# A hand-ordered recurrent scan: the list of pieces rewritten, eight state updates summed on TensorE, zero fills moved to GpSimd

## The chip, the core and the metric

The kernel runs on one core of one Trainium2 chip. The metric is device time in microseconds (us) of one execution. The kernel before took 2023.44 us (median of 3 runs, 2020.06 to 2025.55).

## The reference, cut to what matters

One layer of a diffusion block over 512 latent tokens and 256 context tokens, width 1024. A token mixer runs first (a bidirectional delta-rule scan beside a spatial-gating branch, then gates and an output projection), and an expert-choice mixture of 16 SwiGLU experts after it. The part that is touched is the scan:

```
def step(S, inp):
    r_t, k_t, v_t, d_t, kk_t, a_t = inp
    s_kk = einsum('bhvk,bhk->bhv', S, kk_t)
    S_new = S * d_t - s_kk[..., None] * (kk_t * a_t) + v_t[..., None] * k_t
    y = einsum('bhvk,bhk->bhv', S if reverse else S_new, r_t)
```

It runs forward and backward, 16 heads of 64, first over the context from a zero state, then over the latents from the context's final state.

## The kernel before, in words

The scan is done in chunks of 64 tokens: 4 context steps (0 to 3) and 8 latent steps (4 to 11), each in both directions (d = 0, 1). A step with its direction is written `5.1`. What happens in one step is cut into pieces, each a short function. The order in which all pieces are issued is a string, `PLAN` with its tail `PLAN_END`, read from left to right. The letters:

- `l` (`prep_load`, line 652): loads of the chunk's operands, tiles `al` and `xx`, for both directions; 6 DMAs. In `al` each head pair has a half that must be zero; ScalarE writes it (line 659).
- `S`, `U`, `R` (lines 822 to 840): loads of v into the next state tile `sv` and into `uv`, and of the queries `ro`; 4 DMAs each.
- `a` (`prep`, line 672): 8 products on TensorE; ScalarE copies one part to `ap`, VectorE masks the other part into `al`. `o` stores `ap` to DRAM (4 DMAs).
- `v` (`wave`, line 714) begins a wave, which inverts the triangular blocks of two steps at once: it loads `Dt` from DRAM (the two `o` must have landed) and starts 31 rank-one steps, two VectorE instructions each (`rank1`, lines 710 and 712). `p n` (`pump`) issues n of them, and nothing where no wave is open. `F` issues what is left, and `D` stores the result (a VectorE copy at line 731, 2 DMAs). `i` (`wave_in`) loads it for one step (6 DMAs).
- `V`, `X` (`level`, `level2`): the off-diagonal blocks of the inverse. `K` transposes the keys into `bk`.
- `z`, `y`, `s`: the recurrence. `z` multiplies by the old state (ScalarE copies to `zn`), `y` by the inverse (ScalarE copies to `uv`), `s` gives the next state: TensorE's product is added to `sv` by VectorE (line 882) and scaled by `gC` (line 883), for two halves, so four VectorE instructions.
- `q`, `w`: the chunk's own scores and the outputs, in latent steps only. `h` are parts of the readout that follows.

SP, TensorE and ScalarE work in written order throughout, and within `PLAN` VectorE and GpSimd do as well. All loads are issued by SP's one queue, so a DMA that waits holds back those written behind it. Large tiles share 32 slots (`NBIG`, tag "big"), and a load waits until its slot is free. In the stage ahead of the scan, `HOOK` puts the first five loads, the first two waves and, at its end, `prep_load` 5 between projections. Behind the scan come the branch projections, the router, and then the experts, whose weights (`we`) are streamed from HBM.

A latent pair of steps in the old order reads as follows (step 6 and the start of step 7):

```
y5.0 y5.1 D3 i6 i7 s5.0 a8.0 a8.1 s5.1 o8 w5 l9 U6 V6 K6 X6 S7 z6.1 q6.0 q6.1 z6.0 a9.0 a9.1 o9 v4
R7 y6.0 y6.1 s6.0 s6.1 p8 w6 p4 U7 V7 K7 X7 p4 S8 z7.0 z7.1 p4 q7.0 q7.1 p8 l10 F4 R8 y7.0 y7.1 D4
```

Of the kernel before, what the change touches and what calls it, by code (L numbers as in the profile page):

```python
# [7 lines left out]
F32 = mybir.dt.float32  # L8
F32R = mybir.dt.float32r
I32 = mybir.dt.int32  # L10
AF = mybir.ActivationFunctionType
OP = mybir.AluOpType
# [5 lines left out]
KT = 8  # L18
# [3 lines left out]
C = 64  # L22
# [21 lines left out]
def block_kernel(es: ExitStack, tc, x, ctx, cT, ada_w, ada_b, pc, rows, w_ch, w_vs, w2, a2, g2, sgu_w,  # L44
                 wba, wbb, w_out, rw, e1, e3, e2, out):
    nc = tc.nc
    V, S, G, PE, SY = nc.vector, nc.scalar, nc.gpsimd, nc.tensor, nc.sync

    cp = es.enter_context(tc.tile_pool(name="const", bufs=1))
# [10 lines left out]
    def nm(p):  # L60
        cnt[0] += 1
        return f"{p}{cnt[0]}"

    def T(shape, name="t", dt=F32):
        return big.tile(shape, dt, name=nm(name), tag="big", bufs=NBIG)

    def K(shape, name="t", dt=F32):
        return keep.tile(shape, dt, name=nm(name), tag="keep", bufs=NKEEP)

    def P(name="p"):  # L70
        return pp.tile([128, 512], F32, name=nm(name), tag="ps")

    def mm(o, l, r, start=True, stop=True):
        PE.matmul(o, l, r, start=start, stop=stop, skip_group_check=True)  # L74
# [18 lines left out]
    ident = cp.tile([128, 128], F32, name="ident")  # L93
# [28 lines left out]
    zcol = zcol2[:, 0:1]  # L122
    gC = cp.tile([128, 2, NC, KT], F32, name="gC")

    def rstd(v, n, eps, scale=1.0):
        a = sm.tile([128, n], F32, name=nm("rv"), tag=f"rv{n}")
        y = sm.tile([128, n], F32, name=nm("ry"), tag=f"ry{n}")
        t = sm.tile([128, n], F32, name=nm("rt"), tag=f"rt{n}")
        V.tensor_scalar(a, v, scale, eps, op0=OP.mult, op1=OP.add)  # L129
        V.tensor_scalar(t.bitcast(I32), a.bitcast(I32), 1, None, op0=OP.logical_shift_right)  # L130
        V.tensor_scalar(y.bitcast(I32), t.bitcast(I32), -1, 0x5f3759df, op0=OP.mult, op1=OP.add)
        V.tensor_scalar(a, a, -0.5, None, op0=OP.mult)
        for _ in range(3):
            if n == 1:
                V.scalar_tensor_tensor(t, y, y, a, op0=OP.mult, op1=OP.mult)
            else:
                V.tensor_mul(t, y, y)
                V.tensor_mul(t, t, a)
            V.scalar_tensor_tensor(y, t, 1.5, y, op0=OP.add, op1=OP.mult)
        return y  # L140
# [129 lines left out]
    for d in range(2):  # L270
        for lst, src, nme in ((w2p, w2, "w2p"), (a2p, a2, "a2p")):
            t = T([128, D], nme)
# [34 lines left out]
    for k in range(KT):  # L307
# [5 lines left out]
        for (dst, i0, n, j) in ((hl(k), 2, 4, 0), (hc(k), 0, 2, 1)):  # L313
# [4 lines left out]
            t = T([128, TL], "hf")  # L318
# [314 lines left out]
    def cidx(si, d):  # L633
        lat, s = steps[si]
        n = NCL if lat else NCX
        return lat, (n - 1 - s if d else s)

    def uidx(si, d):
        lat, c = cidx(si, d)
        c += NCX if lat else 0  # L640
        return NC - 1 - c if d else c
# [4 lines left out]
    tmpi = cp.tile([128, 256], F32, name="tmpi")  # L646
    AL, XX, AP_, TP, X1, BK, RO, UV, SV = {}, {}, {}, {}, {}, {}, {}, {}, {}

    def halves(e):
        return (slice(0, 64), slice(64, 128)) if e == 0 else (slice(64, 128), slice(0, 64))  # L650

    def prep_load(si):
        for d in range(2):
            u = uidx(si, d)
            al = T([128, 2, KT, C], "al")
            xx = T([128, KT, 2, C], "xx")
            for e in range(2):
                own, oth = halves(e)
                S.activation(al[oth, e], zcol[oth, :, None].to_broadcast([64, KT, C]), AF.Copy)
                SY.dma_start(al[own, e], Ad_[d, :, own, u, :].rearrange("c p n -> p c n"))  # L660
            SY.dma_start(xx.rearrange("p c s n -> p c (s n)"),
                         Xd_[d, :, :, u].rearrange("c p s n -> p c (s n)"))
            AL[si, d], XX[si, d] = al, xx
# [8 lines left out]
    def prep(si, d):  # L672
        al, xx = AL[si, d], XX[si, d]
        if d == 0:
            AP_[si] = T([128, 2, KT, C], "ap")
        ap = AP_[si][:, d]
        for b in range(2):
            p = P("sc").rearrange("p (c e n) -> p c e n", c=4, e=2)
            for q in range(4):
                ct = 4 * b + q  # L680
                mm(p[:, q], xx[:, ct].rearrange("p s n -> p (s n)"), al[:, :, ct, :])
            cc = slice(4 * b, 4 * b + 4)
            for e in range(2):
                own, oth = halves(e)
                S.activation(ap[own, cc, :], p[own, :, e, :], AF.Copy)
            for e in range(2):
                own, oth = halves(e)
                V.tensor_tensor(al[oth, e, cc, :], p[oth, :, e, :],
                                mS[oth, None, :].to_broadcast([64, 4, C]), OP.mult)
# [162 lines left out]
    yt = [None] * 4  # L852
    QS = {}
# [19 lines left out]
    def state(si, d):  # L873
        bk, sv, uv, svn = BK.pop((si, d)), SV[si, d], UV[si, d], SV[si + 1, d]
        u = uidx(si, d)
        sp = P("sp").rearrange("p (c n) -> p c n", c=KT)
        for ct in range(KT):
            for e in range(2):
                mm(sp[halves(e)[0], ct], bk[:, ct, e, :], uv[:, e, ct, :])
        for e in range(2):  # L880
            own, _ = halves(e)
            V.tensor_tensor(svn[own, e], sp[own], sv[own, e], OP.add)
            V.tensor_tensor(svn[own, e], svn[own, e], gC[own, d, u, :, None].to_broadcast([64, KT, C]), OP.mult)

    def query(si, d):
        xx, ro = XX.pop((si, d)), RO[si, d]
# [10 lines left out]
    def why(si):  # L897
        got = []
        for d in range(2):
            lat, c = cidx(si, d)  # L900
            tt = c // 2
            if yt[tt] is None:
                yt[tt] = K([128, D], "y")
            got.append((RO.pop((si, d)), QS.pop((si, d)), SV.pop((si, d)), UV.pop((si, d)), yt[tt],
                        slice((c % 2) * 64, (c % 2) * 64 + 64), (c < NCL // 2) == (d == 0)))
        for b in range(2):
            ps = [P("yp") for _ in range(2)]
            for q in range(4):
                ct = 4 * b + q
                for e in range(2):  # L910
                    cs = slice(q * 128 + e * 64, q * 128 + e * 64 + 64)
                    for p, (ro, qs, sv, uv, _, hs, _) in zip(ps, got):
                        mm(p[hs, cs], ro[:, e, ct, :], sv[:, e, ct, :], start=True, stop=False)
                    for p, (ro, qs, sv, uv, _, hs, _) in zip(ps, got):
                        mm(p[hs, cs], qs[:, e, ct, :], uv[:, e, ct, :], start=False, stop=True)
            for p, (ro, qs, sv, uv, y, hs, first) in zip(ps, got):
                dst = y[hs, b * 512:b * 512 + 512]
                if first:
                    S.activation(dst, p[hs], AF.Copy)
                else:  # L920
                    V.tensor_tensor(dst, dst, p[hs], OP.add)
# [56 lines left out]
    def finish(_):  # L978
# [7 lines left out]
        ('s', 1): ((prep_load, 2), (pump, 4),),  # L986
        ('b', 0): ((prep_load, 3), (pump, 4),),
        ('a', 1): ((prep_load, 4), (finish, 0),),
        ('end', 0): ((prep_load, 5), (statics, 0),),
        ('u', 5): ((pump, 4),),  # L990
        ('u', 6): ((pump, 4),),
        ('u', 7): ((pump, 4),),
# [65 lines left out]
    for d in range(2):  # L1058
# [1 line left out]
            V.memset(SV[0, d][halves(e)[0], e], 0.0)  # L1060

    PLAN = (
# [9 lines left out]
    ).split()  # L1072
    PLAN_END = (
        "S11 z10.0 z10.1 q10.0 q10.1 h10.0 R11 y10.0 y10.1 s10.0 s10.1 p8 h10.1 w10 h10.2 p4 U11 V11 K11 X11 "
        "p4 z11.0 z11.1 p4 q11.0 q11.1 p8 h11.0 y11.0 y11.1 h11.1 w11 h11.2 "
    ).split()

    def finish_wave(w):
        while gens and waves and gens[0][0] == waves[0][0]:
            pump(1)  # L1080
# [478 lines left out]
    e, hidT = NE - 1, hidTs.pop(NE - 1)  # L1559
# [20 lines left out]
    with tc.manual_schedule():  # L1580
# [9 lines left out]
        r = rstd(mv[:, :, 1], 4, LN_EPS)  # L1590
# [70 lines left out]
```

## Time and profile before

| what | value |
|---|---|
| median of 3 runs | 2023.44 us (2020.06 to 2025.55) |
| the profiled execution, its own time | 2026.06 us |
| its span, first to last instruction | 2024.3 us |
| mean granted TensorE clock | 0.955 of full speed |
| TensorE busy | 1768.7 us (87%), 13216 matmuls |
| VectorE busy | 937.7 us (46%) |
| ScalarE busy | 619.8 us (31%) |
| GpSimd busy | 234.6 us (12%) |
| scan, from the first transposed keys to the last output | 582.0 to 910.8 us |

The span is one execution on the hardware profiler's clock. Busy times of different engines overlap, so they don't sum to the span. In rows of the profile, PE is TensorE, DVE VectorE, ACT ScalarE, POOL GpSimd and SP SyncE, whose queue (SPq) issues the DMAs; "x4" counts instructions, and what stands behind "<-" ended the engine's idle time.

### The profile page before, as it was taken

The numbers are of one execution on the slowest core, as the hardware profiler recorded it, in microseconds if no ns is written. First come the engines' busy times: TensorE is split into PE (matmuls) and PEld (weight loads), VectorE is DVE, ScalarE is ACT, GpSimd is POOL, SyncE is SP. The second block draws the span as 40 slices with busy tenths as digits, with TensorE's granted clock in tenths as the row PEclk, the third lists the DMA queues.
The fourth block names the chain that finished last, engine by engine and source line by source line (L and its number), as shares of the span: only waits on it lengthen the run. The fifth ranks groups of instructions, "written<-read, shape, count | busy, mean of one in ns | idle before, by whom it ended". The sixth has DMA issues, their size and how long they took to land.

```text
span 2024.3 us, 32347 instructions
## 1 busy us (share of the span) xinstructions
PE 1768.7 (87%) x13216; PEld 1134.4 (56%) x13216; DVE 937.7 (46%) x1695; ACT 619.8 (31%) x1057; POOL 234.6 (12%) x158
## 2 busy tenths in 40 slices
PE   5989999899988767687978999999998899999895
PEld 3877778778777767686964443434343243434334
DVE  6788885787836667887782111010201101020115
ACT  2777665443246645352331110100111010011101
POOL 4422224000100000044530000000000000000000
PEclk9999999899999888898978999999999999999998
DMA  9355567477785655484458999999999999999995
GB/s 324 115 172 172 177 189 240 145 229 229 247 234 130 143 135 135 109 235 159 142 232 353 426 427 427 426 427 427 427 427 427 426 427 426 427 427 427 427 424 209
DMA packets 364011, 592.41 MB, mean 293 GB/s; under 512 B 220372, under 2 KB 282068, under 8 KB 315736
## 3 DMA queue, kind: packets, MB, share of 16 engines
q1 hardware_dynamic: 363864, 590.35, 79.0%
q8 instruction: 104, 1.70, 0.3%
q14 instruction: 43, 0.35, 0.1%
HBM read 541.78 MB, written 47.71 MB: 291 GB/s over the span
## 4 chain that ended last, share of the span: by engine, by line
DMA 38%; PE 10%; DVE 4%; issue 0%; ACT 0%; DVEq 0%; SPq 0%
DMA we<-in_e 38%; PE hh L74 4%; PE yx L74 1%; PE co L74 1%; PE ye L74 1%; PE xe L74 1%; PE ba L74 1%; PE lg L74 1%; PE hT L1505 0%; DVE x L1245 0%; DVE wk L1423 0%; DVE m L1422 0%; DVE x L1253 0%; DVE x L1254 0%; DVE mt L1187 0%
## 5 line engine op out<-in xcount | busy, mean ns | idle before, releaser
L74 PE MATMUL hh<-we,xe 128*64 128x512 f32 x2048 | 461.4, 595 | 23.6 <-DMA we<-in_e 23.4
L74 PEld LDWEIGHTS hh<-we,xe 128*64 128x64 f32 x2048 | 149.0, 137 | 322.8 <-issue 261.9
L74 PE MATMUL ye<-we,hidT 128*64 128x512 f32 (+1 forms) x1216 | 253.6, 533 | 37.3 <-DMA we<-in_e 36.9
L1495 DVE TENSOR_TENSOR hd<-hd,hh 64x512 f32<-64x512 f32 x64 | 44.1, 690 | 516.6 <-ACT hd L1494 515.6
L74 PE MATMUL zl<-hL,H 128*128 128x512 f32 x816 | 261.1, 401 | 1.1 <-DVE hf L319 1.1
L74 PEld LDWEIGHTS ye<-we,hidT 128*64 128x64 f32 x1216 | 82.4, 136 | 199.7 <-DMA we<-in_e 106.3
L1494 ACT ACTIVATE hd<-hh 64x512 f32<-64x512 f32 x64 | 37.8, 591 | 490.7 <-PE hh L74 490.7
L74 PEld LDWEIGHTS zl<-hL,H 128*128 128x128 f32 x816 | 155.4, 193 | 30.0 <-issue 2.8
L74 PE MATMUL zl<-hL,L 128*128 128x512 f32 x408 | 163.0, 399 | 9.7 <-DVE L L160 9.7
L160 POOL TENSOR_TENSOR L<-w,H 128x1024 fp32r<-128x1024 f32 x54 | 138.2, 2566 | 208.9 <-ACT H L159 155.2
L159 ACT ACTIVATE H<-w 128x1024 fp32r<-128x1024 f32 x91 | 94.8, 1052 | 83.6 <-PE zl L74 25.1
L1588 POOL TENSOR_TENSOR x<-x,row 128x1024 f32<-128x1024 f32 x2 | 4.6, 2340 | 941.1 <-DVE rv L129 941.1
L1513 ACT ACTIVATE ye<-ye 64x512 f32<-64x512 f32 (+1 forms) x34 | 18.8, 554 | 271.6 <-PE ye L74 271.2
L1514 DVE SCALAR_TENSOR_TENSOR ye<-ye,gate,srow 64x512 f32<-64x512 f32 (+1 forms) x38 | 23.8, 663 | 148.4 <-ACT ye L1513 148.1
L74 PEld LDWEIGHTS zl<-hL,L 128*128 128x128 f32 x408 | 78.6, 193 | 21.8 <-DVE L L160 10.8
L710 DVE TENSOR_TENSOR tmpi<-Dt,Xt 128x31 f32<-128x31 f32 (+15 forms) x186 | 63.6, 342 | 19.7 <-DMA Dt<-Asd 14.1
L712 DVE TENSOR_TENSOR Xt<-Xt,tmpi 128x31 f32<-128x31 f32 (+15 forms) x186 | 63.8, 343 | 6.5
L74 PEld LDWEIGHTS xe<-oh,h 128*128 128x128 f32 x512 | 59.6, 196 | 8.9 <-issue 8.9
L74 PE MATMUL co<-ye,ohT 128*128 128x512 f32 (+1 forms) x144 | 64.4, 604 | 0.0
L74 PE MATMUL sc<-al,xx 128*128 128x128 f32 x384 | 49.6, 289 | 16.3 <-DMA xx<-Xkd 7.9
L74 PE MATMUL xe<-oh,h 128*128 128x128 f32 x512 | 61.8, 282 | 0.7 <-DVE oh L1446 0.7
L160 DVE TENSOR_TENSOR L<-w,H 128x1024 fp32r<-128x1024 f32 x37 | 46.7, 1263 | 31.1 <-ACT H L159 23.8
(322 smaller groups left out, 2914.5 us busy)
## 6 DMA issues: line engine op xcount, KB each, us to landing
we<-in_e SPq DMA_DIRECT2D x376, 1024.0 KB, 19.6
w<-in_w_ch SPq DMA_DIRECT2D x51, 512.0 KB, 4.9
w<-in_ada_w SPq DMA_DIRECT2D x32, 512.0 KB, 5.2
xx<-Xkd SPq DMA_DIRECT2D x28, 512.0 KB, 5.5
adaw<-in_ada_w SPq DMA_DIRECT2D x16, 512.0 KB, 10.3
we<-in_e SPq DMA_DIRECT2D x32, 256.0 KB, 5.5
Xkd<-g SPq DMA_DIRECT2D x32, 192.0 KB, 2.7
Ald<-al SPq DMA_DIRECT2D x16, 384.0 KB, 2.3
```

The lines of the kernel that those rows point to most:

```text
L74: PE.matmul(o, l, r, start=start, stop=stop, skip_group_check=True)
L159: S.activation(h, t, AF.Copy)
L160: (eng or G).tensor_tensor(l, t, h.bitcast(F32), OP.subtract)
L710: V.tensor_tensor(tv, Dt[:, j, None, j + 1:].to_broadcast([128, m, n]), X[:, 0:m, j:j + 1].to_broadcast([128, m, n]), OP.mult)
L712: V.tensor_tensor(X[:, 0:m, j + 1:], X[:, 0:m, j + 1:], tv, OP.subtract)
L1494: S.activation(hd, pn[n][0:64], AF.Silu)
L1495: V.tensor_tensor(hd, hd, pn[n][64:128], OP.mult)
L1513: S.activation(y, p, AF.Copy)
L1514: V.scalar_tensor_tensor(y, p if same else y, gv[e - j][rs], gt2[rs, cs], op0=OP.mult, op1=OP.mult)
L1588: G.tensor_tensor(acc[i], acc[i], l2[0], OP.mult)
```

## The change

The string of pieces is written anew. Pumps are single (`p1`) or in twos and threes between other pieces. Pieces of different steps and directions are mixed, the loads stand further ahead of their use, and load 5 moves from the end of the stage before into the list. In 8 of the 22 updates (`IDENT`) TensorE adds the old state: two products of a 64-column selection matrix with `sv` are accumulated into the same PSUM bank, the line-882 addition goes away, and line 883 reads PSUM. The zero halves of `al` are set by GpSimd's memset in place of ScalarE's copy. `why` no longer drops `sv` and `uv` from their tables, as an update may now stand behind it.

```diff
+    sel = cp.tile([128, 2, 64], F32, name="sel")
+    G.memset(sel, 0.0)
+    for e in range(2):
+        h = slice(e * 64, e * 64 + 64)
+        V.tensor_copy(sel[h, e], ident[h, h])
...
-                S.activation(al[oth, e], zcol[oth, :, None].to_broadcast([64, KT, C]), AF.Copy)
+                G.memset(al[oth, e], 0.0)
...
+        idt = (si, d) in IDENT
+        if idt:
+            for e in range(2):
+                mm(sp[halves(e)[0]], sel[:, e], sv[:, e], True, False)
         for ct in range(KT):
             for e in range(2):
-                mm(sp[halves(e)[0], ct], bk[:, ct, e, :], uv[:, e, ct, :])
+                mm(sp[halves(e)[0], ct], bk[:, ct, e, :], uv[:, e, ct, :], not idt, not idt or ct == KT - 1)
         for e in range(2):
             own, _ = halves(e)
-            V.tensor_tensor(svn[own, e], sp[own], sv[own, e], OP.add)
-            V.tensor_tensor(svn[own, e], svn[own, e], gC[own, d, u, :, None].to_broadcast([64, KT, C]), OP.mult)
+            if not idt:
+                V.tensor_tensor(svn[own, e], sp[own], sv[own, e], OP.add)
+            V.tensor_tensor(svn[own, e], sp[own] if idt else svn[own, e], gC[own, d, u, :, None].to_broadcast([64, KT, C]), OP.mult)
...
-        ('end', 0): ((prep_load, 5), (statics, 0),),
+        ('end', 0): ((statics, 0),),
...
     PLAN = (
+        "t K0 V0 z0.0 z0.1 a4.0 p1 X0 V1 p1 y0.1 l5 a5.0 p1 a5.1 p1 a4.1 p2 S1 s0.1 i2 r y0.0 o5 p1 X1 V2 z1.1 p2 "
+        "s0.0 o4 K1 U1 p2 v2 p3 y1.1 z1.0 S2 p7 X2 y1.0 p1 s1.1 p2 s1.0 i3 S3 V3 K3 p2 z2.1 p1 K2 U2 R4 y2.1 l6 "
+        "p1 z2.0 p1 S4 R5 p1 K4 p1 X3 F2 D2 s2.1 y2.0 p1 K5 s2.0 a6.0 U3 a6.1 p1 z3.1 q5.0 y3.1 l7 z3.0 o6 q4.1 "
+        "y3.0 p1 q5.1 s3.1 a7.0 a7.1 i4 V4 p3 s3.0 X4 z4.1 q4.0 o7 p3 i5 p1 v3 p1 z4.0 p2 V5 p2 U4 y4.1 X5 p2 S5 "
+        "y4.0 p3 s4.1 s4.0 w4 p1 l8 U5 p3 R6 l9 z5.0 S6 p3 z5.1 y5.0 K6 p1 y5.1 F3 D3 p1 i6 p2 s5.0 p1 a8.0 w5 K7 "
+        "p1 a8.1 a9.0 a9.1 z6.0 p1 o8 p1 s5.1 U6 q6.1 p1 i7 p2 V6 p3 q6.0 X6 p1 o9 R7 z6.1 y6.0 S7 p3 y6.1 p1 v4 "
+        "s6.0 S8 V7 s6.1 p1 q7.0 X7 z7.1 p1 q7.1 p3 U7 y7.1 z7.0 p2 w6 p3 l10 p5 s7.1 p2 l11 p1 S9 p2 y7.0 a10.0 "
+        "w7 p2 z8.1 p1 K8 R8 R9 U8 F4 D4 a10.1 p1 a11.0 p1 a11.1 q8.0 p1 o10 K9 q9.0 i8 s7.0 V8 q8.1 o11 q9.1 v5 "
+        "p1 z8.0 p5 X8 p1 y8.0 p1 U9 p1 i9 p1 y8.1 s8.1 p1 U10 p4 w8 R10 S10 S11 V9 s8.0 z9.1 p1 K10 F5 D5 q10.0 "
+        "z9.0 X9 p1 K11 y9.1 i10 p3 y9.0 "
     ).split()
     PLAN_END = (
+        "q10.1 p1 s9.1 U11 s9.0 w9 V10 h10.0 z10.1 X10 z10.0 p1 y10.1 h10.1 y10.0 p5 s10.1 R11 s10.0 p4 w10 p2 "
+        "i11 p1 z11.0 h10.2 p1 V11 p1 q11.1 X11 z11.1 h11.0 y11.0 q11.0 p3 y11.1 p2 h11.1 w11 h11.2 "
     ).split()
+    IDENT = {(1, 0), (4, 0), (4, 1), (7, 1), (8, 0), (8, 1), (9, 1), (10, 1)}
```

## Rows read from the trace of the kernel before

**Rows 1.** The page: its span, and the chain that ended last by line
```profile
span 2024.3 us, 32347 instructions
DMA we<-in_e 38%; PE hh L74 4%; PE yx L74 1%; PE co L74 1%; PE ye L74 1%; PE xe L74 1%; PE ba L74 1%; PE lg L74 1%; PE hT L1505 0%; DVE x L1245 0%; DVE wk L1423 0%; DVE m L1422 0%; DVE x L1253 0%; DVE x L1254 0%; DVE mt L1187 0%
```

**Rows 2.** Stretches: length, busy PE, PEld, DVE, ACT, POOL, then clock, DMA share, GB/s
```profile
400.00:582.00 182.00, 177.13 (x822) 144.53 (x821) 137.57 (x237) 64.30 (x97) 12.00 (x18) 0.99 0.73 234
582.00:620.30 38.30, 29.35 (x667) 26.98 (x667) 14.01 (x27) 27.74 (x59) 1.12 (x2) 0.96 0.72 166
620.30:662.40 42.10, 31.79 (x782) 29.35 (x776) 33.21 (x79) 29.02 (x60) 0.00 (x0) 0.92 0.56 121
662.40:700.00 37.60, 28.28 (x673) 26.79 (x673) 20.73 (x42) 19.20 (x42) 1.11 (x2) 0.87 0.71 156
700.00:727.00 27.00, 17.96 (x325) 17.00 (x320) 24.87 (x72) 12.69 (x26) 0.00 (x0) 0.87 0.50 119
727.00:762.60 35.60, 27.55 (x646) 25.89 (x648) 20.55 (x42) 18.29 (x38) 1.11 (x2) 0.90 0.71 160
762.60:789.60 27.00, 19.68 (x422) 18.56 (x416) 24.87 (x72) 16.82 (x35) 0.00 (x0) 0.98 0.51 124
789.60:826.30 36.70, 28.96 (x665) 27.28 (x666) 20.66 (x42) 17.60 (x38) 1.11 (x2) 0.88 0.70 155
826.30:856.00 29.70, 17.91 (x426) 16.99 (x423) 27.49 (x76) 8.58 (x17) 0.00 (x0) 0.84 0.27 61
856.00:910.80 54.80, 44.83 (x989) 42.16 (x989) 45.06 (x82) 27.16 (x55) 20.53 (x11) 0.90 0.86 231
1073.00:2024.00 951.00, 869.17 (x4272) 361.29 (x4272) 140.72 (x261) 92.82 (x159) 4.64 (x2) 0.98 0.98 411
```

**Rows 3.** VectorE's timeline: a wave's first rank-one step and its closing copy
```profile
762.58 0.19 DVE L710 TENSOR_TENSOR tmpi<-Dt,Xt 128x31 f32<-128x31 f32 x1
788.60 1.02 DVE L731 COPY Dt<-Xt 64x1024 f32<-64x1024 f32 x1
```

**Rows 4.** Groups of instructions from 582 to 912: busy us, mean ns | idle before
```profile
L882 DVE TENSOR_TENSOR sv<-sp,sv 64x512 f32<-64x512 f32 x44 | 30.3, 688 | 19.9 <-PE sp L74 10.8 <-DMA sv<-Vd 5.2 <-ACT uv L871 3.2
L688 DVE TENSOR_TENSOR al<-sc,mS 64x256 f32<-64x256 f32 x64 | 27.0, 422 | 27.5 <-ACT ap L685 26.3
L895 DVE TENSOR_TENSOR qs<-qs,mF 128x256 f32<-128x256 f32 x32 | 11.7, 418 | 24.6 <-PE qs L74 24.0
L850 ACT ACTIVATE bk<-bk 128x512 f32<-128x512 f32 x48 | 25.2, 601 | 5.6 <-DMA Gd<-ga 4.1 <-PE bk L849 0.9 <-DMA Mo<-mod 0.2
```

**Rows 5.** TensorE's timeline, pieces of step 7: start us, us, count of instructions
```profile
761.74 1.21 PE L74 MATMUL l<-x,ap 128*32 128x32 f32 x64
762.88 1.97 PE L849 MATMUL bk<-ident,xx 128*128 128x128 f32 x16
771.84 2.09 PE L74 MATMUL up<-zn,tp 128*64 128x64 f32 x64
```

**Rows 6.** The chain of waits, in order of time: an expert's products
```profile
1083.30 3.58 PE hh L74 x16
```

**Rows 7.** SP's timeline: issue start us, us, line
```profile
589.33 2.01 SPq L660 DMA_DIRECT2D al<-Ald  x2
...
727.05 0.48 SPq L732 DMA_DIRECT2D Xpd<-Dt  x1
...
757.21 0.34 SPq L716 DMA_DIRECT2D Dt<-Asd  x1
```

**Rows 8.** SP's waits in the scan: us in total, times, longest
```profile
SPq L732 <- DVE Dt L731: 61.3, 4, 22.2
```

**Rows 9.** Timeline: GpSimd's memset and VectorE's scaling (L883) beside GpSimd
```profile
605.45 0.96 POOL L718 MEMSET Xt<- 128x1024 f32 x1 [25.33 <-PE sp L74]
606.20 0.69 DVE L883 TENSOR_TENSOR sv<-sv,gC 64x512 f32<-64x512 f32 x1
...
882.79 2.71 DVE L883 TENSOR_TENSOR sv<-sv,gC 64x512 f32<-64x512 f32 x2
```

More of the change, by code (lines that the diff above doesn't have):

```diff
@@ L903, in why @@
                 yt[tt] = K([128, D], "y")
-            got.append((RO.pop((si, d)), QS.pop((si, d)), SV.pop((si, d)), UV.pop((si, d)), yt[tt],
+            got.append((RO.pop((si, d)), QS.pop((si, d)), SV[si, d], UV[si, d], yt[tt],
                         slice((c % 2) * 64, (c % 2) * 64 + 64), (c < NCL // 2) == (d == 0)))
@@ L1062, in block_kernel @@
     PLAN = (
[9 rows of a table removed]
[10 rows of a table added]
     ).split()
     PLAN_END = (
-        "S11 z10.0 z10.1 q10.0 q10.1 h10.0 R11 y10.0 y10.1 s10.0 s10.1 p8 h10.1 w10 h10.2 p4 U11 V11 K11 X11 "
-        "p4 z11.0 z11.1 p4 q11.0 q11.1 p8 h11.0 y11.0 y11.1 h11.1 w11 h11.2 "
+        "q10.1 p1 s9.1 U11 s9.0 w9 V10 h10.0 z10.1 X10 z10.0 p1 y10.1 h10.1 y10.0 p5 s10.1 R11 s10.0 p4 w10 p2 "
+        "i11 p1 z11.0 h10.2 p1 V11 p1 q11.1 X11 z11.1 h11.0 y11.0 q11.0 p3 y11.1 p2 h11.1 w11 h11.2 "
     ).split()
+    IDENT = {(1, 0), (4, 0), (4, 1), (7, 1), (8, 0), (8, 1), (9, 1), (10, 1)}
     def finish_wave(w):
```

9 rows, old and new, of the table PLAN are left out of this document.

## The prediction

> **What bounds the kernel now.** I read the page first: the chain that ended last is mostly the expert weights [rows 1], and from 1073 on the DMA engines are at 0.98 [rows 2]. That stage has its own limit, but it starts only when the scan and the projections behind it free the memory it loads into. Whatever the scan loses or gains therefore moves the end one for one, and 1113.5 us of the span (910.8 to 2024.3) stay as they are.
>
> Then I cut the scan at VectorE's marks: the first rank-one step of each wave, and the closing copy (D). That gives nine stretches, which I call A to I (the second to the tenth line of [rows 2]): A 38.3, B 42.1, C 37.6, D 27.0, E 35.6, F 27.0, G 36.7, H 29.7, I 54.8; together 328.8 us. In B, D, F and H a wave runs. The reader is to see that VectorE is at 92% in D, F and H (24.87 of 27.0, 27.49 of 29.7) and TensorE is not. In C, E and G no wave runs, VectorE is busy 20.5 to 20.7 us and TensorE 27.6 to 29.0 of 36 to 38, so neither is full. There I looked at SP: from the stores of one wave (727.05) to the load of the next (757.21) it issues 36 DMAs in 30.2 us, 0.84 us each with their small waits, and the first rank-one step follows 5.4 us later, when that load has landed [rows 3, 7]. So the path is: D, SP's queue, `Dt`, next wave. SP also stands 61.3 us, in four goes, waiting for the closing copies [rows 8]: time in which it could issue what stands behind.
>
> **The change, part by part.** Prices. A wave is 26.0 us from first step to copy [rows 3] with one step's `q` inside, 8 x 0.418 = 3.3 [rows 4]: 22.7 alone. An update is 4 x 0.69 = 2.8 us of VectorE, with TensorE's addition 2 x 0.69 = 1.4 [rows 4]. An `a` is 4 x 0.42 = 1.7, a `q` 1.7 per direction [rows 4]. On TensorE `V` or `X` costs 1.2, `K` 2.0, and one direction of `z` or `y` 2.09/2 = 1.05 [rows 5].
>
> *TensorE's additions.* The trace has no such product. The nearest row is an expert's: 64 columns, 512 wide, both halves of the array, 16 instructions in 3.58 us [rows 6]; two of them make one product, so 0.45 us, and an update's two products 0.9. Below, it is nothing, where it fits into TensorE's wait for `uv`; above, twice that, 1.8, if the two halves don't overlap. I take 0.9, as the row has both halves in it. Six of the eight lie in B, D, F and H, which VectorE bounds; two in I: 1.8 us. The gain: 1.4 us of VectorE each.
>
> *The zero fills.* 20 lie before the scan, where TensorE is busy 177 of 182 us and ScalarE 64 [rows 2]: nothing. The other 28 leave ScalarE, busy at most 27.7 of 38.3 us, and go to GpSimd, which has 1 us of work per stretch [rows 2]. I take nothing; if GpSimd's queue were full, each would delay a load's use by 0.5 us (half of the 0.96 us for 1024 columns [rows 9]).
>
> A row speaks against this. Beside a GpSimd operation the scaling at line 883 took 2.71 us for two, in place of 1.4, but beside a memset 0.69 for one [rows 9]. The Trainium skill (SBUF — State Buffer, "SBUF: two separate sides") says that GpSimd and VectorE share one pair of ports under an exclusive lock; VectorE operations with two SBUF inputs contend only with a GpSimd operation that reads SBUF. By that rule a memset, which reads nothing, is harmless, and the 0.69 agrees; the sum stays as it is. If the lock held for memsets too, the time would be that of rival 3.
>
> *The order*, stretch by stretch. SP's DMAs are counted from the list (`l` 6, `S`, `U`, `R`, `o` 4, `i` 6, `D` 2). A `p` without an open wave does nothing, so in A, C, E and G the single steps written there are void. Of each wave 16 to 23 steps are spread, and F issues the rest.
>
> - A. Load 5 now stands behind K0, so four slots are free, and `bk` needn't wait for the gate's store (4.1 us [rows 4]). SP comes free at 589.3 [rows 7], then has load 5, S1, i2, o5, o4, U1 ahead of v2: 28 x 0.84 = 23.5, plus 5.4: first step at 618.2. A = 36.2 (−2.1).
> - B. Step 2's updates move behind D2, step 1's second one loses its additions: 22.7 + 2.8 + 1.4 + copy 1.0 = 27.9. VectorE had stalls here in the old order, among them 5.2 us for a `sv` load [rows 4]; S2 and S3 now stand well ahead. (−14.2)
> - C. D2, U3, l7, o6, i4, o7, i5: 32 x 0.84 = 26.9, plus 5.4 = 32.3 (−5.3). VectorE has 2 x 5.6 for updates, 4 x 1.7 for `a`, 4 x 1.7 for `q`: 24.8, below it.
> - D. 22.7 + 2.8 (step 4, both with TensorE's addition) + 1.0 = 26.5 (−0.5). SP: 32 x 0.84 = 26.9, a tie.
> - E. 34 DMAs, 28.6 + 5.4 = 34.0 (−1.6). VectorE: updates 11.2, `a` 6.8, `q` 3.4 = 21.4.
> - F. 22.7 + `q` 3.3 + 1.4 + `a` 1.7 + 1.0 = 30.1 (+3.1); SP 36 x 0.84 = 30.2, a tie.
> - G. Only D4, o10, i8, o11 remain ahead of v5, as l11, S9, R8, R9 and U8 went to F: 16 x 0.84 + 5.4 = 18.8 (−17.9). VectorE: 3 `a`, 4 `q`, one update: 14.7.
> - H. 22.7 + 2.8 + outputs 2.8 + 1.0 = 29.3 (−0.4).
> - I. Compared with the old list TensorE has X9, one `z`, two `y` and two additions more (1.2 + 1.05 + 2.1 + 1.8) and K10 less (2.0): +4.2; K11 needs only loaded keys and can run during the last rank-one steps (−2.0): 57.0 (+2.2).
>
> Sum: 292.1 us, 36.7 less. The profiled execution took 2026.06 us, 1.8 more than its span and 2.6 more than the median; 2026.1 − 36.7 = 1989.4 for it, **1987** for the median. The moved cost is in F and I: what the old order did between waves is now beside them.
>
> **The rivals.**
> 1. *More.* The 5.4 us for `Dt` stay on the path in A, C, E and G by my sum. If VectorE has enough other pieces left there, they vanish: 21.6 us more, 1965. For it: E and C hold 21 to 25 us of such work. Against: the list puts most of it ahead of `v`.
> 2. *Half.* G's gain comes from loads moved into F. The slots: counted over the list (first use to last), the new order has 31 to 33 large tiles alive at S1, l7, S6, S9, U8, U9, U10 and S11, where 32 exist; the old has at most 27 from step 3 on. If F's loads wait for slots, G's 17.9 are paid in F: 2005. For it: F is at SP's limit already, without a wait. Against: tiles of step 6 go free early in F.
> 3. *GpSimd blocks VectorE.* 28 fills x 0.5 us = 14 us: 2001. The 0.69 us [rows 9] speaks against it.
> 4. *Slower: SP becomes the bound through the slots.* SP is one in-order queue; a load that waits for a slot holds every `i`, `o` and `v` behind it. Eight loads stand at the limit. From 36.7/8 = 4.6 us of wait at each the gain is gone, from 5.4 on it is slower. A slot goes free at the end of a `z`, `y`, `s` chain; on engine times alone one chain is 3 x 1.05 on TensorE, 4 copies of about 0.6 on ScalarE [rows 4] and 2.8 on VectorE, 8.4 us. If every one waits that long: 67 − 36.7 = 30 slower, 2053. For it: SP's 0.84 us leaves no room. Against: the 61.3 us in which SP waits for copies [rows 8] are room, if the waits fall there.
> 5. *The order's gains are given back in waits that I don't see*, in PSUM banks or on ScalarE, of some 3 to 5 us in each stretch: about 2023.
>
> **How the numbers follow.** My forecast 0.43; more 0.14; half 0.23; GpSimd 0.06; given back 0.06; slower 0.08. About 0.3% (6 us) is what a measurement of this kernel can tell from no change. Faster then holds 0.86, same 0.06, slower 0.08. The range from 1965 (rival 1) to 2013 (half the gain, and 8 us of small waits) leaves out the last two cases and a little at the low end. The addition's bounds (0 to 1.8 us, twice in I) move it by 2.
>
> **What would show it.** Right: B near 28 and G near 19 us between the marks, F a little longer than 27; no wait over 3 us of SP for a slot; 28 line-882 instructions in place of 44 (30.3 to 19 us); memsets of 0.5 us without longer line-883 instructions; 1113 us behind the scan. Wrong: SP idle on `PE` or DVE releasers at loads in F, or line 883 near 1.4 us each beside a memset; or a stretch C or E longer than 38 us. If the stage behind the scan changes by more than 5 us, my first step (one for one) fails.

## The result, and the profile after

The changed kernel takes 1994.68 us (median of 4 runs, 1992.99 to 1997.92); the kernel before took 2021.75 us beside it (4 runs, 2018.74 to 2025.55). The ratio is 0.9867, 95% interval 0.9844 to 0.989: 27 us less. Forecast were 1987 us, with 1965 to 2013 as the range.

Line numbers of the scan move by 6 to 11: the zero fill is L665, the mask L694, a wave's rank-one step L716 and L718, its load L722, its closing copy L737 with the store L738, loads of v L825 and L826, the update's addition L893 and its scaling L894, the scores L906, the expert weights L1453.

The page of the changed kernel, its span and the chain that ended last by line, answers to [rows 1]: the expert weights still end the program.

```profile
span 1991.0 us, 32397 instructions
DMA we<-in_e 41%; PE hh L74 3%; PE yx L74 1%; PE co L74 1%; PE ye L74 1%; DVE x L1258 1%; PE lg L74 1%; PE xe L74 0%; DMA w<-in_wba 0%; DVE mt L1200 0%; DVE x L1266 0%; DVE mgL L1204 0%; PE hT L1518 0%; DVE wk L1436 0%; DVE m L1435 0%
```

The same cuts as in [rows 2], A to I and the expert stage, for the changed kernel (length, busy PE, PEld, DVE, ACT, POOL, clock, DMA share, GB/s):

```profile
583.30:619.36 36.06, 30.16 (x789) 28.43 (x789) 12.17 (x24) 27.93 (x62) 7.34 (x14) 0.95 0.83 185
619.36:648.02 28.66, 18.17 (x424) 16.46 (x420) 26.38 (x69) 15.90 (x33) 2.08 (x4) 0.91 0.73 165
648.02:684.93 36.91, 34.55 (x734) 32.81 (x735) 23.38 (x49) 20.97 (x46) 5.27 (x10) 0.93 0.61 136
684.93:712.06 27.13, 17.99 (x418) 15.78 (x414) 24.93 (x67) 13.37 (x27) 2.07 (x4) 0.92 0.85 207
712.06:746.89 34.83, 31.14 (x720) 29.87 (x720) 20.52 (x41) 18.30 (x41) 1.97 (x4) 0.91 0.62 133
746.89:777.47 30.58, 28.29 (x572) 26.51 (x564) 27.91 (x77) 19.89 (x42) 3.30 (x7) 1.00 0.78 189
777.47:794.03 16.56, 14.23 (x260) 12.85 (x262) 13.21 (x32) 5.65 (x13) 1.11 (x2) 0.90 0.75 165
794.03:824.03 30.00, 19.62 (x496) 16.91 (x496) 27.68 (x71) 11.47 (x24) 0.00 (x0) 0.88 0.45 96
824.03:881.02 56.99, 50.19 (x1213) 46.36 (x1213) 40.42 (x77) 26.54 (x53) 20.27 (x11) 0.94 0.80 216
1040.00:1991.00 951.00, 867.79 (x4272) 361.06 (x4270) 140.24 (x258) 92.71 (x159) 4.64 (x2) 0.98 0.98 410
```

Set beside the forecast, stretch by stretch (us):

| | A | B | C | D | E | F | G | H | I | scan |
|---|---|---|---|---|---|---|---|---|---|---|
| before | 38.3 | 42.1 | 37.6 | 27.0 | 35.6 | 27.0 | 36.7 | 29.7 | 54.8 | 328.8 |
| forecast | 36.2 | 27.9 | 32.3 | 26.5 | 34.0 | 30.1 | 18.8 | 29.3 | 57.0 | 292.1 |
| after | 36.1 | 28.7 | 36.9 | 27.1 | 34.8 | 30.6 | 16.6 | 30.0 | 57.0 | 297.7 |

B and G give 13.4 and 20.1 us, F costs 3.6. One stretch is far from its term, C, with 4.6 us.

Groups of instructions of the changed scan (busy us, mean ns | idle before) answer to [rows 4]. The additions fall from 44 to 28, the scaling that reads PSUM (`sv<-sp`) costs as much as the one that reads SBUF, and the 16 selection products (32 instructions) take 8.5 us.

```profile
L893 DVE TENSOR_TENSOR sv<-sp,sv 64x512 f32<-64x512 f32 x28 | 19.3, 688 | 13.5 <-PE sp L74 12.9
L894 DVE TENSOR_TENSOR sv<-sv,gC 64x512 f32<-64x512 f32 x28 | 19.2, 686 | 0.9
L894 DVE TENSOR_TENSOR sv<-sp,gC 64x512 f32<-64x512 f32 x16 | 11.0, 687 | 1.4 <-PE sp L74 1.2
L665 POOL MEMSET al<- 64x512 f32 x28 | 14.5, 519 | 118.5 <-PE zp L74 35.9 <-PE l L74 33.7 <-PE yp L74 16.9
L74 PE MATMUL sp<-sv,sel 128*64 128x512 f32 x32 | 8.5, 600 | 0.0
```

The wave in F answers to [rows 3]: VectorE's first step and closing copy in the changed kernel, now 30.6 us apart with the moved scores in between.

```profile
746.89 0.19 DVE L716 TENSOR_TENSOR tmpi<-Dt,Xt 128x31 f32<-128x31 f32 x1
...
776.44 1.03 DVE L737 COPY Dt<-Xt 64x1024 f32<-64x1024 f32 x1
```

SP's waits in the whole changed scan (us in total, times, longest) answer to [rows 8]. The wait for closing copies is 20.3 in place of 61.3: SP now does other work in that time. The last line is new: a load of `uv` that stood 5.5 us for its slot.

```profile
SPq L738 <- DVE Dt L737: 20.3, 3, 12.1
SPq L703 <- ACT ap L691: 6.6, 5, 4.5
SPq L825 <- PE sp L74: 5.5, 1, 5.5
```

That wait lies in C. SP's timeline of the changed kernel there (start, us; whole lines, others left out) and VectorE's first step of the next wave, with what it waited for:

```profile
648.06 0.49 SPq L738 DMA_DIRECT2D Xpd<-Dt  x1
648.65 0.53 SPq L739 DMA_DIRECT2D Xsd<-Xt  x1
654.78 0.52 SPq L825 DMA_DIRECT2D uv<-Vd  x1
...
680.31 1.15 SPq L722 DMA_DIRECT2D Dt<-Asd  x1
```

```profile
684.93 0.19 DVE L716 TENSOR_TENSOR tmpi<-Dt,Xt 128x31 f32<-128x31 f32 x1 [4.28 <-DMA Dt<-Asd]
```

From the store to the load of the next `Dt` SP needs 32.3 us; less the gap of 5.6 it would be 26.7, and the forecast had 26.9. In size this one wait would explain C, but a run below takes it away and C stays as long. What held the slot is read on TensorE, whose timeline has the transposition of step 5's keys (`K5`) standing 9.12 us for the VectorE update just before, and behind it, in written order, the products of `s2.0` that free the `uv` slot:

```profile
650.32 3.30 PE L855 MATMUL bk<-ident,xx 128*128 128x128 f32 x16 [9.12 <-DVE sv L893]
653.55 1.15 PE L74 MATMUL sp<-uv,bk 128*64 128x64 f32 x32
```

GpSimd's and VectorE's timelines of the changed kernel answer to [rows 9]: two memsets run from 678.00 to 679.09, and the scaling that starts at 678.11 takes its usual 0.69 us.

```profile
678.00 1.09 POOL L665 MEMSET al<- 64x512 f32 x2 [4.88 <-PE zp L74]
```

```profile
678.11 0.69 DVE L894 TENSOR_TENSOR sv<-sv,gC 64x512 f32<-64x512 f32 x1
```

### The profile page after: what moved, and what is told of

Same layout as the page of the kernel before. It is cut to its first block, busy times and chain, and to the rows that moved or that the text cites. A ratio compares the mean times of both kernels' runs of the same rounds, so it can differ in the third digit from the quotient of the medians.

```text
span 1991.0 us, 32397 instructions
## 1 busy us (share of the span) xinstructions
PE 1768.8 (89%) x13248; PEld 1130.4 (57%) x13248; DVE 924.9 (46%) x1681; ACT 589.9 (30%) x1009; POOL 260.5 (13%) x207
## 4 chain that ended last, share of the span: by engine, by line
DMA 41%; PE 8%; DVE 5%; issue 1%; POOL 0%; ACT 0%; DVEq 0%; SPq 0%; POOLq 0%; ACTq 0%
DMA we<-in_e 41%; PE hh L74 3%; PE yx L74 1%; PE co L74 1%; PE ye L74 1%; DVE x L1258 1%; PE lg L74 1%; PE xe L74 0%; DMA w<-in_wba 0%; DVE mt L1200 0%; DVE x L1266 0%; DVE mgL L1204 0%; PE hT L1518 0%; DVE wk L1436 0%; DVE m L1435 0%
## 5 line engine op out<-in xcount | busy, mean ns | idle before, releaser
L74 PE MATMUL ye<-we,hidT 128*64 128x512 f32 (+1 forms) x1216 | 254.0, 533 | 37.2 <-DMA we<-in_e 36.9
L1526 ACT ACTIVATE ye<-ye 64x512 f32<-64x512 f32 (+1 forms) x34 | 18.8, 553 | 271.5 <-PE ye L74 271.2
L716 DVE TENSOR_TENSOR tmpi<-Dt,Xt 128x31 f32<-128x31 f32 (+15 forms) x186 | 63.6, 342 | 14.6 <-DMA Dt<-Asd 8.9
L718 DVE TENSOR_TENSOR Xt<-Xt,tmpi 128x31 f32<-128x31 f32 (+15 forms) x186 | 63.8, 343 | 6.5
L74 PEld LDWEIGHTS zc<-hC,H 128*128 128x128 f32 x288 | 54.0, 188 | 12.7 <-POOL hC L321 0.4
L160 DVE TENSOR_TENSOR L<-w,H 128x1024 fp32r<-128x1024 f32 x37 | 46.1, 1245 | 30.3 <-ACT H L159 28.7
```

What stands on the lines that cost most here:

```text
L160: (eng or G).tensor_tensor(l, t, h.bitcast(F32), OP.subtract)
L716: V.tensor_tensor(tv, Dt[:, j, None, j + 1:].to_broadcast([128, m, n]), X[:, 0:m, j:j + 1].to_broadcast([128, m, n]), OP.mult)
L718: V.tensor_tensor(X[:, 0:m, j + 1:], X[:, 0:m, j + 1:], tv, OP.subtract)
L1526: S.activation(y, p, AF.Copy)
```

## The experiments

Stretches are cut in each kernel's own trace by the same marks. Ratios are to the kernel before on the same chip, with 95% intervals.

### The order alone

Without TensorE's additions, fills on ScalarE: what is left of the change is the list.

```diff
-    IDENT = {(1, 0), (4, 0), (4, 1), (7, 1), (8, 0), (8, 1), (9, 1), (10, 1)}
+    IDENT = set()
-                G.memset(al[oth, e], 0.0)
+                S.activation(al[oth, e], zcol[oth, :, None].to_broadcast([64, KT, C]), AF.Copy)
```

> The new order alone: no update has its old state added by TensorE, the zero fills are on ScalarE again. My theory (the order carries nearly all of the gain, since it sets what stands ahead of each wave): VectorE gets 6 x 1.4 us back in the stretches that a wave bounds, TensorE loses 1.8 us in I: 6 to 8 us above the changed kernel, ratio to before 0.990. Rival (the additions and the fills carry it, the order little): above 2012 us, ratio over 0.995.

2004.6 us, ratio 0.991 (0.9896 to 0.9925). Two thirds of the gain (18 of 27 us) are the order's. B is 30.1 and G 16.5 without any addition on TensorE. C is 41.5, with the fills on ScalarE (see the run with the fills alone).

### Without the additions on TensorE

Only `IDENT = set()`; the fills stay on GpSimd.

> The changed kernel with no addition on TensorE (16 VectorE additions back, 32 matmuls fewer). Theory: B, D, F, H grow by 1.4, 2.8, 1.4, 2.8 us, I falls by up to 2: +6 us. Rival a (TensorE is the bound everywhere): 0 or below, as 8.5 us of TensorE go away. Rival b (the additions sit on the recurrence in every stretch): +11 us or more.

2003.92 us, ratio 0.9908 (0.9894 to 0.9923): 9 us slower than the changed kernel. B, D, F and H are 30.1, 30.0, 31.4 and 32.9 here, against 28.7, 27.1, 30.6 and 30.0: 8.0 us together, where six additions at 1.4 make 8.4. I is 56.8 against 57.0: there, where TensorE sets the pace, moving an addition to it is worth nothing. C and E are longer here too (40.4 and 37.4), but neither holds an addition in either kernel, and both differ by as much between kernels whose lists are alike there, so I don't ascribe that.

### The fills back on ScalarE

Only the second pair of lines above; the additions stay on TensorE.

> The changed kernel with the zero fills on ScalarE. Theory: ScalarE has room, 0 to 2 us. Rival (the fills stand in ScalarE's queue ahead of copies of the recurrence, 28 x 0.63 us): +10 to +17 us. If GpSimd's memsets held VectorE's ports, this would be faster than the changed kernel by up to 14 us.

1992.29 us, ratio 0.985 (0.9834 to 0.9866), against 0.9867 with the fills on GpSimd. The intervals overlap: the fills are worth nothing that can be measured in the time here. It is the lowest time of all runs. The rival that GpSimd blocks VectorE foresaw 14 us to be won by taking the memsets away. It falls.

In the scan the fills are not free on ScalarE. In C four of them stand ahead of a copy to `zn` that TensorE waits for:

```profile
666.52 2.55 ACT L665 ACTIVATE al<-zcol 64x512 f32<-64x512 f32 x4
```

```profile
669.74 0.33 PE L74 MATMUL up<-zn,tp 128*64 128x64 f32 x2 [1.56 <-ACT zn L867]
```

C is 41.7 us in place of 36.9 and the scan 301.1 in place of 297.7; 1.8 of these 3.4 us come back behind the scan, and the profiled executions differ by 1.4.

### The old order with the rest

The list of before with TensorE's additions and GpSimd's fills.

```diff
-    PLAN, PLAN_END: the new list
+    PLAN, PLAN_END: the list of before
-        ('end', 0): ((statics, 0),),
+        ('end', 0): ((prep_load, 5), (statics, 0),),
```

> The old order (load 5 at the end of the stage before again) with the 8 additions on TensorE and the fills on GpSimd. Theory: none of the 8 updates stands inside a wave in the old order but step 1's; a few us at most: -2 (0 to -5), ratio 0.998 to 1.000. Rival (these two edits carry the gain): -15 us or more.

2028.88 us, ratio 1.0034 (1.0022 to 1.0047): slower. The scan itself is shorter, 321.0 us against 328.8, in C (33.6 for 37.6) and G (33.3 for 36.7). In C VectorE still waits 3.58 us for `Dt` when its updates are done, so its shorter updates are not what ended C sooner; what did was not tested. The gain does not reach the end. SP's waits behind the scan (1000 to 1100) in this kernel:

```profile
SPq L1452 <- PE lg L74: 34.4, 1, 34.4
```

An expert load stood 34.4 us for a slot that a router product (`lg`) held. From 1020 to 1045 nothing was streamed here (first line: windows of this kernel; below it the kernel before, where the DMA engines were at 0.69).

```profile
1020.00:1045.00 25.00, 19.07 (x105) 17.68 (x103) 18.39 (x67) 5.03 (x12) 2.23 (x1) 0.66 0.00 1
```

```profile
1020.00:1045.00 25.00, 21.83 (x115) 19.33 (x113) 21.75 (x54) 3.48 (x7) 9.83 (x4) 0.78 0.69 280
```

TensorE's first expert product (`hh`: count, ns min/median/max, first and last start), here, and below it in the kernel before and in the changed kernel:

```profile
L74 PE MATMUL hh<-we,xe x2048: 592/592/1057, 1069.0 to 1955.9; 128*64 128x512 f32 x187
```

```profile
L74 PE MATMUL hh<-we,xe x2048: 592/592/1116, 1076.8 to 1957.7; 128*64 128x512 f32 x187
```

```profile
L74 PE MATMUL hh<-we,xe x2048: 592/592/1116, 1043.2 to 1924.5; 128*64 128x512 f32 x187
```

From first to last it is 886.9 us here, 880.9 before and 881.3 after: the stage starts 7.8 us earlier and takes 6.0 longer. The likeliest reason is that idle stretch of the stream: the tuned kernel below has such a stretch too, and the same 886.9 us. It was not tested by itself. So a gain in the scan does not pass through to the end in every order. That the timed runs are 7 us above before, and not merely level as this one execution (span 2023.7), is not explained by the trace.

### The loads alone, in the old order

The kernel before, with four pieces of loads moved out of stretch G: into the wave ahead of it, or behind the next wave's load.

```diff
-        "... p8 l10 F4 R8 y7.0 y7.1 D4 "
-        "i8 i9 s7.0 s7.1 a10.0 a10.1 o10 w7 l11 U8 V8 K8 X8 S9 z8.0 z8.1 q8.0 q8.1 a11.0 a11.1 o11 v5 R9 y8.0 "
+        "... p8 l10 l11 F4 R8 U8 y7.0 y7.1 D4 "
+        "i8 s7.0 s7.1 a10.0 a10.1 o10 w7 V8 K8 X8 z8.0 z8.1 q8.0 q8.1 a11.0 a11.1 o11 v5 i9 S9 R9 y8.0 "
```

> The old order with one thing of the new: l11 and U8 stand ahead of F4 D4, i9 and S9 behind v5, so 20 fewer DMAs lie between D4 and the load of wave 5. Theory (SP's queue sets G): G falls from 36.6 towards TensorE's 29 us of work there, by 5 to 8 us, F stays at 27: 2014 to 2017 us, ratio 0.996 to 0.998. Rival (G is set by the chain of TensorE and VectorE pieces and only their new order shortens it): 0, ratio 1.000.

2018.22 us, ratio 0.9981 (0.9967 to 0.9994). G is 31.7 in place of 36.7, and F stays at 27.0. So SP's queue is part of what bounds G, but the moved loads alone give 5 of the 20 us that G lost in the change. As many DMAs stand ahead of `v5` here as in the changed kernel, 16, and yet G is 31.7 us and not 16.6, since SP stands and waits for the part of step 11 that `o11` stores:

```profile
SPq L697 <- ACT ap L685: 14.1, 1, 14.1
```

The new list issues `a11` right behind D4. The rest is thus VectorE's and TensorE's work, which it takes out of G ahead of that store (VectorE 20.66 to 13.21 us, TensorE 28.96 to 14.23).

### Twelve more DMAs, in E or in H

Twelve loads of 4 KB into a spare tile that nothing reads, issued by SP between two waves (E, ahead of `v4`) or during a wave (H, behind `v5`).

```diff
+    spare = cp.tile([128, 12, 8], F32, name="spare")
+    def extra(_):
+        for k in range(12):
+            SY.dma_start(spare[:, k], pc[:, 8 * k:8 * k + 8])
-        "... S7 p3 y6.1 p1 v4 "
+        "... S7 n0 p3 y6.1 p1 v4 "
```

> The changed kernel with 12 small extra DMAs on SP's queue between D3 and the load of wave 4 (they load 32 bytes per partition into a tile that nobody reads). Theory (SP sets E): E grows by 12 x 0.4 to 0.6 = 5 to 7 us. Rival (TensorE, busy 31 of 34.8 us, sets E): 0 to 2 us.

> The same 12 extra DMAs right behind the load of wave 5, in H, where VectorE is busy 27.7 of 30.0 us. Theory: 0 to 1 us. Rival (SP is the bound everywhere): 5 to 7 us.

With the DMAs in E, 2017.97 us, ratio 0.9981 (0.9968 to 0.9994); in H, 2013.23, ratio 0.9954 (0.9932 to 0.9976). E grows from 34.6 to 42.7 us between the two, 8.1 for twelve DMAs or 0.68 each, and H is 30.0 in the changed kernel and in both of these. In E the whole of it is VectorE's wait for `Dt` (waits of the kernel with the DMAs in E, 714 to 762); in the changed kernel that wait isn't there.

```profile
DVE tmpi L716 <- DMA Dt<-Asd: 8.1, 1, 8.1
```

So in E SP's queue stands level with TensorE without slack, and in H it has room for at least twelve more. But both kernels are slower than the scan explains: with the DMAs in H the scan is 306.2 us, 8.5 above the changed kernel's, and the time 18.5 above. The rest came from the experts, and this I had not expected in either theory.

### The changed kernel once more, a tuned version, and K5 moved

> The changed kernel once more, beside the others on the same chip: ratio 0.985 to 0.988, and a second profile, which tells how much a single stretch varies from one execution to the next (I expect 1 us, C perhaps 4).

1994.63 us, ratio 0.9857 (0.9838 to 0.9876), with stretches within 1.2 us of the first profile (C 38.1).

To test the reading of C, `K5` goes from C into D, behind `s4.1` (and `query` no longer drops `xx` from its table, as `K5` now stands behind it):

```diff
-        s2.1 y2.0 p1 K5 s2.0 a6.0 ... y4.0 p3 s4.1 s4.0 w4
+        s2.1 y2.0 p1 s2.0 a6.0 ... y4.0 p3 s4.1 K5 s4.0 w4
```

> The changed kernel with K5 alone moved from C into D. Theory (C is TensorE's, busy 34.6 of 36.9 us, after a wait of 9 us for a PSUM bank ahead of K5): C falls by 3 us or more, D stays at 27. Rival, my prediction's term (SP's 32 DMAs and the landing of Dt set C): C stays at 37 to 38.

1995.31 us, ratio 0.9869 (0.9851 to 0.9886): no change. (Its profiled span, 2002.1, is above these times; I read only C from it, 36.9 us as before.) SP's waits in C of this kernel:

```profile
SPq L703 <- ACT ap L691: 4.8, 1, 4.8
SPq L825 <- PE l L74: 0.8, 2, 0.6
```

The slot wait is gone, as `K5` explains it; but SP now stands 4.8 us for step 7's `ap` (the stores of `o7`), and `Dt` is loaded 32.0 us after the store, as before. My reading of the slot was right, and undoing it was worth nothing. What holds C is seen when `o7` is set beside the last products of `a7` (`sc<-al,xx`), first in the changed kernel, then in this one:

```profile
669.60 3.84 PE L74 MATMUL sc<-al,xx 128*128 128x128 f32 x32
673.88 3.13 SPq L703 DMA_DIRECT2D Asd<-ap  x4
```

```profile
670.26 3.84 PE L74 MATMUL sc<-al,xx 128*128 128x128 f32 x32
674.54 1.90 SPq L703 DMA_DIRECT2D Asd<-ap  x4
...
682.14 0.42 SPq L722 DMA_DIRECT2D Dt<-Asd  x1
```

In both SP starts these stores 0.4 us after the products end, 25.9 and 24.4 us after the closing copy. So TensorE's chain of pieces up to `a7` sets them (TensorE is busy 34.71 us of 36.9 here), and the six issues of `i5` stand between them and the load of `Dt`.

A version with this, `v2` ahead of `K1 U1`, `v3` ahead of `i5`, and the additions in another choice of steps:

```diff
-        s0.0 o4 K1 U1 p2 v2 p3 y1.1 ... o7 p3 i5 p1 v3 p1 z4.0
+        s0.0 o4 p2 v2 K1 U1 p3 y1.1 ... o7 p3 v3 i5 p1 p1 z4.0
+    IDENT = {(1, 0), (1, 1), (4, 0), (4, 1), (7, 1), (8, 0), (8, 1)}
```

> The changed kernel, tuned by what the runs before show: K5 moved from C into D, where TensorE has room; K1 and U1 behind v2 and i5 behind v3, so that fewer DMAs stand ahead of a wave's load; the additions of steps 9 and 10 back on VectorE (I is TensorE's stretch) and step 1's second one on TensorE (B is VectorE's). Theory: A -1, B -1.4, C -3, I 0 to -1: 5 us below the changed kernel, ratio to before 0.983. Rival (slots decide: whatever moves, loads wait for the same tiles): ratio 0.986 as it is now, or above.

1997.82 us, ratio 0.9884 (0.9869 to 0.99): no better. A to C shrink by 5.4 us together (0.7, 1.4 and 3.2, about as the theory had it), D, E and F grow by 5.7, and the scan is 298.1 us. What leaves C is due again in the next stretches. C is 33.7 us here. `o7` starts 24.2 us after the closing copy, as with `K5` moved alone, and the load of `Dt`, without `i5` ahead of it, follows at 29.2 in place of 32.0:

```profile
668.92 1.90 SPq L703 DMA_DIRECT2D Asd<-ap  x4
673.89 0.34 SPq L722 DMA_DIRECT2D Dt<-Asd  x1
```

That the time is 3 us above the changed kernel's comes from behind the scan. An expert load stands 23.5 us for a slot that `lg` held (the longest such wait of the changed kernel is 8.5), and the experts' `hh` products take 886.9 us from first to last, as with the old order and the rest:

```profile
SPq L1453 <- PE lg L74: 23.5, 1, 23.5
```

```profile
L74 PE MATMUL hh<-we,xe x2048: 592/592/1116, 1040.9 to 1927.8; 128*64 128x512 f32 x187
```

### The spare tile by itself

The changed kernel with the spare tile of 384 bytes per partition, written once, and none of the DMAs; then the same with 256 bytes.

```diff
+    spare = cp.tile([128, 12, 8], F32, name="spare")     # 384 bytes; [128, 8, 8]: 256 bytes
+    V.memset(spare, 0.0)
```

> The changed kernel with a tile of 384 bytes per partition in the constant pool, written once and never read; no extra DMA. It shifts the addresses of the large tiles. In the two runs with extra DMAs, which had that tile, the expert weights came at 421 GB/s instead of 427. Theory (the address does it): 421 GB/s, expert stage 935 us instead of 923, ratio 0.992 to 0.995. Rival (the extra DMAs did it): 427 GB/s, 923 us, ratio 0.986.

> The changed kernel plus a constant tile of 256 bytes per partition that nothing reads. With one of 384 bytes the expert weights came at 421 GB/s in place of 427 and the time was 2011.3 us. Theory: what matters is by how many bytes the tiles allocated behind it are moved, and a move by 256 is different from one by 384: weights at 427 GB/s again, time near 1995. Rival: any extra tile, or any move at all, costs the 1.4%: 421 GB/s, an expert stage of about 935 us from its first product to its last, time near 2011. The scan is expected the same in both, 298 to 303 us.

With 384 bytes 2011.33 us, ratio 0.995 (0.9936 to 0.9964); with 256 bytes 1994.14, ratio 0.9877 (0.9853 to 0.9901), as without the tile. The expert stage from 1120 to 1920, first with 384 bytes, then with 256 (last column GB/s), and its first products:

```profile
1120.00:1920.00 800.00, 731.27 (x3442) 300.12 (x3440) 101.62 (x174) 76.50 (x129) 0.00 (x0) 0.99 1.01 421
```

```profile
1120.00:1920.00 800.00, 742.20 (x3494) 299.43 (x3492) 101.67 (x174) 76.62 (x129) 0.00 (x0) 0.99 1.01 427
```

```profile
L74 PE MATMUL hh<-we,xe x2048: 592/592/1117, 1050.6 to 1943.0; 128*64 128x512 f32 x187
```

```profile
L74 PE MATMUL hh<-we,xe x2048: 592/592/1113, 1041.9 to 1922.2; 128*64 128x512 f32 x187
```

892.4 us against 880.3. The kernels with twelve DMAs show the same 421 GB/s and, with the DMAs in E, 892.6 us. So 11 to 12 us of their expert stage belong to the tile and not to the DMAs. Against the kernel with the tile alone (2011.33) the DMAs cost 6.6 us in E and 1.9 in H, and the difference between E and H is what those two runs tell.

## Why the prediction was right, point by point

- **The path.** "D, SP's queue, `Dt`, next wave" held in A, C and G, where VectorE waits 3.16, 4.28 and 1.45 us for `Dt`. In G the load is issued 12.6 us after the store, where 16 x 0.84 made 13.4, and the step follows 3.9 us later, not 5.4: 16.6 for 18.8. But the 16 issues alone don't give this: with as many the old order's G was 31.7, and SP stood 14.1 us for the stores of step 11. My term for G had no such wait and came near because the new list also has `a11` early; that part is luck. In E VectorE did not wait for `Dt`; TensorE (31.14 of 34.83 us) and SP arrive together, and the twelve DMAs show that SP is level there. I got E's 34.0 from SP alone.
- **B.** 28.7 us for 27.9. VectorE's work there fell from 33.2 to 26.4 us and its idle time from 8.9 to 2.3; the 5.2 us wait for a `sv` load is gone. It is the order's: with the old order and the rest B is 43.0.
- **C.** The step that failed. The term counted issues and no wait, and assumed that slots would be free. A slot wait of 5.5 us came in, but without it C is 36.9 us as well. The path that the term left out is TensorE's: the products of `a7` end 25.4 us after the closing copy (24.0 with `K5` moved), `o7` starts 0.4 us later, and only then come `i5` and the load of `Dt`. In C TensorE's busy time rose from 28.28 to 34.55 us; the prediction added up VectorE and SP there, and not TensorE.
- **The additions.** 16 products took 8.5 us, 1.06 us for an update, where the experts' products [rows 6] had given 0.9. 8.0 us in four stretches against 8.4, and nothing in I. I came out at its term, 57.0 us, but the 1.8 us for two additions in it did not show: with them back on VectorE it is 56.8.
- **The fills.** 0.519 us each, nothing on the path. The rule that I weighed (the Trainium skill, SBUF — State Buffer, "SBUF: two separate sides") agrees here for a memset. It bears on the 28 scalings with two SBUF inputs; their mean is 0.686 us, and the three that can be seen to run beside a memset (at 629.09, 678.11 and 746.08) took 0.69 each. The row of before [rows 9] was weak evidence: memset and scaling overlapped for 0.21 us.
- **F and the slots.** F is 30.6 (30.1). SP's slot waits in F were 2.4 us at the most, so what the rival "half" foresaw, that the moved loads are paid in F, did not come. Its mechanism showed once, in C, at 5.5 us; the slower rival needed it at all eight loads. My own bound for being wrong, a slot wait of over 3 us, was met there, in a stretch that is 4.6 us over its term, and it did not cost the gain.
- **The other rivals.** Of "more", the landing of `Dt` vanished from the path in E alone, where TensorE took its place. "Given back" came in the size of C's 4.6 us, not of the 3 to 5 us in each stretch that it needed.
- **One for one.** 1110.0 us lie behind the scan, against 1113.5. It held for this change, within the 5 us, but it is no law: the old order with the additions and the fills lost 6.0 of 7.8 us behind the scan, and the tuned kernel 5.6.
- **The sum.** The profiled execution took 1992.99 us where 1989.4 was forecast: 1.3 us later start, 5.6 in the scan (4.6 in C), 3.5 less behind it, 0.2 outside the span. The other 4.3 us between 1987 and 1994.68 are the choice of executions: before, the profiled one lay 2.6 us above the median, after, 1.7 below.

Open: why C differs by up to 5 us between kernels with the same pieces there is answered in part. It is 36.9, 38.1 and 38.2 us in three with the changed list and the fills on GpSimd. With the fills on ScalarE (41.7) the products of `a7` end 30.0 us after the closing copy in place of 25.4. Without the additions (40.4) they end at 25.6, but VectorE's step comes 6.6 us after the issue of the load of `Dt` in place of 4.6, and why is open. So are the mechanism of the 384 bytes and what the idle stretch of the expert stream costs.

## What to carry to other kernels

In a scan whose order is written by hand, count each stretch between two marks for every engine and for the issuing queue: the queue's sum gave G to 2 us, but only as the products that its stores wait for came early too, and in C, where TensorE's chain to such a store had been left out, it was wrong. So ask of each store in the queue's count when its data are ready. Move work off the engine that bounds a stretch, and only there: an addition moved to TensorE was worth 1.4 us in a wave and nothing at the end. Before a gain in an early stage is counted in full, look at what the next stage's first transfers wait for.

## What the runs showed of the hardware

A constant tile of 384 bytes per partition, which nothing reads and which moves what is allocated behind it, took the expert weights from 427 to 421 GB/s (1.4%) and the kernel from 1994.7 to 2011.3 us; 256 bytes left both as they were (427 GB/s, 1994.1 us). The change's own `sel` is such a tile too, of 512 bytes, and the rate is 427 GB/s before and after it. It looks as if the rate depends on where the tiles of the weights lie; why 384 and not 256 or 512 is open, and no other size was run. A spare tile is thus not a neutral control, and an experiment that adds one has to run the tile by itself.
